# Two middle feed-forwards of a decoder trunk: from two column groups to one, with seven block products

## The chip, the cores and the metric

One core of a Trainium2 chip runs the whole kernel in one launch. The metric is device time in microseconds (us) of that core, the median of three runs.

## The reference, cut to what matters

Two layers, each feed-forward, token mixer, feed-forward, on 512 tokens of width 1024. Each sub-layer is normed, and scaled, shifted and gated by rows of a modulation that is computed from a vector `c`. All in float32.

```python
c_act = jax.nn.silu(c)
for l in range(DEPTH):                                  # DEPTH = 2
    mod = (c_act @ w_ada[l] + b_ada[l]).reshape(B, N_MOD, D_MODEL)
    sh1, sc1, gt1, sh2, sc2, gt2, sh3, sc3, gt3 = [mod[:, i, None, :] for i in range(N_MOD)]
    hn = rms_norm(h, g_ffn1[l]) * (1.0 + sc1) + sh1
    h = h + 0.5 * (1.0 + gt1) * swiglu(hn, w_ffn1_in[l], w_ffn1_out[l])
    ...                                                 # the mixer, with sh2, sc2, gt2
    hn = rms_norm(h, g_ffn2[l]) * (1.0 + sc3) + sh3
    h = h + 0.5 * (1.0 + gt3) * swiglu(hn, w_ffn2_in[l], w_ffn2_out[l])

def swiglu(x, w_in, w_out):                             # w_in 1024 x 5632, w_out 2816 x 1024
    gate, up = jnp.split(x @ w_in, 2, axis=-1)
    return (jax.nn.silu(gate) * up) @ w_out
```

The order of the sub-layers is ffn1, mix, ffn2 of layer 0, then ffn1, mix, ffn2 of layer 1, numbered n = 0 to 5. The two "middle" feed-forwards are n = 2 and n = 3, which follow each other without a mixer between.

## The kernel before

Everything is held transposed: features on the 128 partitions, tokens along the free axis. `h` is 8 tiles of 128 x 512. The normed input `hn` is 8 pairs of tiles (`hnH`, `hnL`), high and low part of each value: a float32 product is made of three matmuls in a faster format (H by H, H by L, L by H; `mm3`, `mm6`, `prod`), which accumulate in PSUM. A weight block of 128 x 1024 is loaded as `wraw`, and `split` (L103 to L105) makes `wH` by a cast on ScalarE (ACT) and `wL` by a subtraction on VectorE (DVE). `wH` and `wL` have four buffers each.

A feed-forward has 2816 = 22 x 128 inner columns, numbered j. The first four of them (in n = 0 the first eight) are computed tile by tile (`projector`), and meanwhile sums and differences of `hn` halves (P1, P2, T3, T4) are prepared. The others go in pairs p (two j each, `pair_in`): gate and up of both are made by seven block products of 24 matmuls of 256 columns in the place of eight, on sums of weight blocks. These sums come partly from DVE and partly from transfers that add to what lies in SBUF (`plus`, issued on GpSimd's (POOL) queue). Plain weight loads go through SyncE's (SP) queue.

Feed-forwards n = 0, 2 and 3 run in two groups of inner columns (`GROUPS`, 12 and 10). After each group its part of the out product is computed, eight tiles of 12 and 10 row blocks by 512 tokens, and added to `h` by DVE (`residual`). The last two tiles of the second group are computed in halves of 256 tokens by `close`, with the next norm's statistics between them, lower half of the tokens first; DVE and ACT have a fixed order there.

The last feed-forward, n = 5, runs in one group (`whole_k`): the products of the pairs are kept in `raw` tiles, and the out product is computed by seven block products (`out_strassen`, matmuls at L661) of 11 row blocks, 4 tiles and 3 matmuls, 256 columns each. Some of its weight sums come from accumulating transfers (L565), some from DVE (L606), and `finish` (L668) adds the products to `h`.

The modulation is computed by the way. `ada_steps` loads a row block of `w_ada` (512 KB) on POOL's queue, and DVE multiplies and sums it against a replicated silu(c), called `crep` (`ada_dot`, L168, a "dot" below). Each middle feed-forward computes 36 dots, 21 beside the out product of group 0 and 15 beside that of group 1; the last one computes 8, each in two halves, beside its pairs. `crep` is loaded and passed through silu in each feed-forward.

The order of instructions on each engine is found by a list scheduler from the program order; `issue_after` adds constraints, and within `manual_schedule` the named engines keep the program order. The wait of an instruction stops all that is behind it on its engine or queue.

Of the kernel before, what the change touches and what calls it, by code (L numbers as in the profile page):

```python
# [35 lines left out]
GROUPS = ((0, 12), (12, 22))  # L36
RWKV_WORK, ATT_WORK, FILL_WORK = 29.8, 15.2, 129.6
# [23 lines left out]
def trunk_kernel(ctx, tc, ins, out, layers=L, phases=("ffn1", "mix", "ffn2")):  # L61
# [107 lines left out]

    def ada_crep(pool):  # L170
        c = pool.tile([P, D], F32, name="crep", tag="crep", bufs=1)
        nc.sync.dma_start(c, ins["crep"])
        act(c, c, AF.Silu)
        return c

    def ada_steps(pool, crep, n, behind=None):
# [16 lines left out]
        del todo[:n]  # L193

# [23 lines left out]
    def norm(l, g, ish, isc, ss):  # L218
# [18 lines left out]
        def spread(sl):  # L237

            r, pt = rstd[sl.start], psum([P, T // 2], "ps_rstd", "r0" if sl.start else "x")
            for b in range(2):  # L240
                mm(pt[:, b * P : (b + 1) * P], r[:, b : b + 1].to_broadcast([P, P]), cst("ident"), start=True, stop=True)
            rstd[sl.start] = pt
# [20 lines left out]
    loads = []  # L263

# [15 lines left out]
    def projector(srcs, hn, tags, pts=None, ahead=0, ready=None):  # L280
# [8 lines left out]
        if pts is None:  # L289
            pts = [psum([P, T], "ps_mm", tag) for tag in ("mm", "mm", "r1")]  # L290
            for sl in HALVES:
                for k in range(KD):
                    for w, pt in zip(ws, pts):
                        mm3(pt[:, sl], w, k, hn[k], sl, k == 0 and sl is HALVES[0], k == KD - 1 and sl is HALVES[1])
# [77 lines left out]
    def ffn(l, w_in, w_pair, w_out, hn, im, ss, need, then, ready, first=None, late=None):  # L372
# [6 lines left out]
        with tc.tile_pool(name="act", bufs=1) as ap_:  # L379
# [3 lines left out]
            whole_k = ss is None  # L383
# [26 lines left out]
            raws_ = []  # L410

            def new_raw():
                raws_.append(ap_.tile([P, 2, 2, T], F32, name="raw", tag="raw", bufs=6))
                return raws_[-1]

            def corner(X):
                return tt(X[:, 0, hi_], X[:, 1, hi_], X[:, 0, hi_], ALU.subtract)

            def new_x(p):

                if whole_k:
                    return (new_raw() if p % 2 == 0 else raws_[-1])[:, p % 2]
# [6 lines left out]
            free_rows = [new_raw()[:, i] for _ in range(2) for i in range(2)] if whole_k else []  # L429
            raws_.clear()  # L430

            def whole(n):

                for k in (2 * n, 2 * n + 4):
                    x = free_rows.pop(0) if whole_k else ap_.tile([P, 2, T], F32, name="x", tag="act", bufs=12)
# [36 lines left out]
            def put(X, sl, x, y):  # L472
                if whole_k:
                    done_ = tt(X[:, :, sl], x, y, ALU.mult)
                    return corner(X) if sl is hi_ else done_
                tt(x, x, y, ALU.mult)
# [3 lines left out]
            def pair_in(p):  # L480
# [55 lines left out]
                put(X, hi_, up, s2)  # L536

                def rest(between=None):
                    prod(pD, hl(raw(A(1, 1), None, "last")), T4, False)
                    if between:  # L540
                        between()
                    return put(X, lo_, gate, pD)

                waiting.append(rest)

            def out_strassen(rest, raws):

                cg = small_.tile([P, KD], F32, name="cg", tag="cg")
                for c, v in ((slice(0, 4), -0.5), (slice(4, 8), 0.5)):
                    ts(cg[:, c], mod[l, im + 2][:, c], v, v, ALU.mult, ALU.add)  # L550
                pD, pF, pG = ([psum([P, 2, H2], n, t) for _ in range(2)] for n, t in (("ps_d", "x"), ("ps_f", "mm"), ("ps_g", "r0")))
                ws, NU = ins["w2s"], len(raws)
                tall = [slice(2 * u, min(2 * u + 2, NF // 2)) for u in range(NU)]
                size = [s.stop - s.start for s in tall]
                S_, ready_ = {}, {}

                def block(u, *names):
                    return ws[names[0], names[1], :, tall[u]].rearrange("p k m c -> p (k m) c")

                chain = {}  # L560

                def queued(eng, op, *args, **kw):
                    last = chain.get(eng)
# [1079 lines left out]
```

## Time and profile before

| | |
|---|---|
| runs | 1884.96, 1885.17, 1879.71 us; median 1884.96 |
| the profiled execution | 1883.92 us, span 1881.8 us, granted TensorE clock 0.999 |
| TensorE matmul (PE) | busy 99% of the span |
| TensorE weight load (PEld) | 92% |
| VectorE (DVE) | 78% |
| ScalarE (ACT) | 46% |
| GpSimd (POOL) | 8% |
| moved by DMA | 317.19 MB, mean 169 GB/s |

A busy time is that in which an engine executed something; matmuls overlap in the pipeline, and so the distance between the starts of two of them tells more than the mean duration of one. The DMA share is the mean busy share of the core's 16 DMA engines. A stretch is a piece of the span for which the profile sums all of this.

### The profile page before, as it was taken

The page shows a single profiled execution, that of the slowest core. Times are in us where ns is not written, and L with a number is a line of the kernel's source. Part 1 is how long each engine was busy: PE and PEld are TensorE (multiplying, and loading weights), DVE is VectorE, ACT ScalarE, POOL GpSimd, SP SyncE. Part 2 cuts the span into 40 slices and gives each one's busy share as a digit, 9 for nine tenths or more (in the row PEclk, how much of TensorE's full clock was granted, in tenths as well). Part 3 has the DMA queues.
Part 4 walks back from the last instruction along what each step waited for, and adds up shares of the span by engine and source line. Part 5 has one row for each costly group of instructions (what it writes and reads, how often), then busy time and mean ns, then how long its engine had stood idle before and what let it go on. Part 6 is the DMA issues. An engine that isn't in the chain of part 4 may idle for free.

```text
span 1881.8 us, 37923 instructions
## 1 busy us (share of the span) xinstructions
PE 1853.7 (99%) x15796; PEld 1733.0 (92%) x15796; DVE 1462.8 (78%) x2320; ACT 871.5 (46%) x1312; POOL 155.9 (8%) x243
## 2 busy tenths in 40 slices
PE   9999999999999999999999999999999999999999
PEld 8998899897889999899899989999878889999999
DVE  7787687858886877678787776878498768888996
ACT  4453355346432555245345524544554335555653
POOL 0101100100000010110100011110000000111120
PEclk9999999999999999999999999999999999999999
DMA  8667877521222285886817688782211315787855
GB/s 305 245 180 235 261 200 235 169 71 46 75 60 71 90 228 167 291 221 188 278 56 204 174 270 234 190 267 83 91 53 60 94 39 160 213 226 210 234 129 141
DMA packets 110028, 317.19 MB, mean 169 GB/s; under 512 B 23968, under 2 KB 29088, under 8 KB 108832
## 3 DMA queue, kind: packets, MB, share of 16 engines
q1 hardware_dynamic: 78192, 203.33, 31.6%
q0 software_dynamic: 31664, 111.43, 24.2%
q8 instruction: 124, 2.03, 0.4%
q14 instruction: 48, 0.39, 0.1%
HBM read 311.31 MB, written 3.41 MB: 167 GB/s over the span
## 4 chain that ended last, share of the span: by engine, by line
PE 83%; DVE 11%; ACT 2%; issue 2%; DMA 2%; SPq 0%; ACTq 0%; DVEq 0%
PE ps_mm L101 16%; PE ps_mm L94 8%; PE ps_mm L93 8%; PE ps_mm L95 8%; PE ps_d L467 7%; PE ps_d L469 6%; PE ps_d L468 6%; PE ps_f L469 3%; PE ps_f L467 3%; PE ps_f L468 3%; PE ps_d L661 2%; PE ps_g L469 2%; PE ps_g L467 1%; PE ps_g L468 1%; PE ps_f L661 1%
## 5 line engine op out<-in xcount | busy, mean ns | idle before, releaser
L104 ACT CAST wH<-wraw 128x1024 fp32r<-128x1024 f32 (+3 forms) x266 | 249.1, 940 | 402.0 <-PE ps_mm L94 102.2
L105 DVE TENSOR_TENSOR wL<-wraw,wH 128x1024 fp32r<-128x1024 f32 (+3 forms) x266 | 286.6, 1081 | 69.2 <-ACT wH L104 68.6
L467 PE MATMUL ps_d<-comH,wH 128*128 128x256 f32 x816 | 226.1, 277 | 1.2 <-ACT s L511 0.7
L468 PE MATMUL ps_d<-comL,wH 128*128 128x256 f32 x816 | 225.3, 276 | 0.0
L469 PE MATMUL ps_d<-comH,wL 128*128 128x256 f32 x816 | 225.2, 276 | 0.0
L93 PE MATMUL ps_mm<-actH,wH 128*128 128x512 f32 (+1 forms) x588 | 216.5, 368 | 0.0
L94 PE MATMUL ps_mm<-actL,wH 128*128 128x512 f32 (+1 forms) x588 | 216.0, 367 | 0.0
L95 PE MATMUL ps_mm<-actH,wL 128*128 128x512 f32 (+1 forms) x588 | 216.0, 367 | 0.0
L168 DVE SCALAR_TENSOR_TENSOR wada<-wada,crep 128x1024 f32<-128x1024 f32 (+1 forms) x148 | 169.4, 1162 | 48.1 <-DMA wada<-in_wadaT 47.8
L101 PE MATMUL ps_mm<-hnH,wL 128*128 128x256 f32 x976 | 199.5, 282 | 1.0 <-DVE wL L105 1.0
L101 PE MATMUL ps_mm<-hnH,wH 128*128 128x256 f32 x976 | 197.4, 282 | 0.6 <-ACT wH L104 0.3
L101 PE MATMUL ps_mm<-hnL,wH 128*128 128x256 f32 x976 | 197.2, 280 | 0.0
L104 ACT CAST wH<-sum 128x1024 fp32r<-128x1024 f32 x122 | 128.5, 1054 | 139.1 <-PE ps_d L468 66.4
L105 DVE TENSOR_TENSOR wL<-sum,wH 128x1024 fp32r<-128x1024 f32 x122 | 149.1, 1223 | 54.6 <-ACT wH L104 54.5
L101 PEld LDWEIGHTS ps_mm<-hnH,wL 128*128 128x128 f32 x976 | 149.5, 188 | 8.5 <-issue 6.6
L101 PEld LDWEIGHTS ps_mm<-hnH,wH 128*128 128x128 f32 x976 | 148.7, 188 | 8.5 <-issue 5.1
L467 PEld LDWEIGHTS ps_d<-comH,wH 128*128 128x128 f32 x816 | 153.2, 188 | 2.6 <-ACT s L511 1.7
L101 PEld LDWEIGHTS ps_mm<-hnL,wH 128*128 128x128 f32 x976 | 149.5, 188 | 5.2 <-issue 4.9
L468 PEld LDWEIGHTS ps_d<-comL,wH 128*128 128x128 f32 x816 | 153.2, 188 | 0.0
L469 PEld LDWEIGHTS ps_d<-comH,wL 128*128 128x128 f32 x816 | 153.2, 188 | 0.0
L95 PEld LDWEIGHTS ps_mm<-actH,wL 128*128 128x128 f32 x588 | 110.9, 189 | 18.3
L93 PEld LDWEIGHTS ps_mm<-actH,wH 128*128 128x128 f32 x588 | 110.9, 189 | 18.2
(474 smaller groups left out, 4716.4 us busy)
## 6 DMA issues: line engine op xcount, KB each, us to landing
wada<-in_wadaT POOLq DMA_DIRECT2D x120, 512.0 KB, 5.1
wraw<-in_wmi SPq DMA_DIRECT2D x40, 512.0 KB
wraw<-in_w2p SPq DMA_DIRECT2D x36, 512.0 KB
wraw<-in_w1p SPq DMA_DIRECT2D x32, 512.0 KB
wraw<-in_w1o SPq DMA_DIRECT2D x32, 384.0 KB
wraw<-in_w1i SPq DMA_DIRECT2D x20, 512.0 KB
wraw<-in_w1o SPq DMA_DIRECT2D x32, 320.0 KB
sum<-in_w2p SPq DMA_DIRECT2D x18, 512.0 KB
```

Of the source, the lines that this page charges most:

```text
L93: mm(acc, wH, xH, start=start, stop=False)
L94: mm(acc, wH, xL, start=False, stop=False)
L95: mm(acc, wL, xH, start=False, stop=stop)
L101: mm(acc[:, sl], w[a][:, k], x[b][:, sl], start=start and n == 0 and sl is HALVES[0], stop=stop and n == 2, skip_group_check=True)
L104: nc.scalar.copy(hi, src)
L105: return nc.vector.tensor_sub(lo, src, hi.bitcast(F32))
L168: stt(w, w, 1.0, crep, ALU.mult, ALU.mult, accum_out=out_)
L467: mm(pt[:, i], wH, x[k][0], start=start and i + k == 0, stop=False, skip_group_check=True)
L468: mm(pt[:, i], wH, x[k][1], start=False, stop=False, skip_group_check=True)
L469: last = mm(pt[:, i], wL, x[k][0], start=False, stop=k == 3, skip_group_check=True)
L661: mm(pt[m // 2][:, m % 2], w[:, 4 * k + m], x[:, y, k], start=start and u + k + n + m % 2 == 0, stop=u == NU - 1 and n == 2, skip_group_ch ...
```

## The change

Feed-forwards n = 2, 3 and 5 get a function of their own, `ffn_whole`; n = 0 keeps `ffn`, from which the code for one group is removed.

- All pairs come first, the out product last, in seven block products as in `out_strassen`. The first product is now copied by ACT from its PSUM tile into that of the third, and the sixth into that of the seventh, which accumulate on it; their separate additions to `h` go.
- In `pair_in` the a00 product is copied by ACT into the PSUM tile of the third product (which accumulates on it), in place of an addition by DVE. The loaded block a00 itself becomes the third weight sum by an accumulating transfer, in place of a second load. The order of the last two products is changed.
- The dots go to fixed places, by the table `DOTS`: in n = 2 and 3 six beside the first tiles, then 4, 4, 4, 4, 4, 4, 3, 2, 1 beside pairs 2 to 10; in n = 5 two beside each of pairs 2 to 5. Their rows go to parts of the `raw` tiles that are free at the time (`ROWS`), and a load is issued as soon as a dot has freed a buffer, up to a pair ahead.
- silu(c) is stored to DRAM once at the start (`silu_c`), and each feed-forward loads it from there.
- At the end of n = 2 and 3 the fixed order of DVE and ACT is written anew: the next norm's upper half is applied beside the last units of the seventh product, the lower half behind it, and the next stage's first tiles start with the upper half (`lead`).

The core of the diff:

```diff
+DOTS = ((0, 0, 2, 2, 2, 2), (0, 6, 4, 4, 4, 4, 4, 4, 3, 2, 1))
+ROWS = {1: (0, 1, 2, 3), 2: (0, 1, 2, 3), 3: (0, 1, 2, 3), 4: (2, 3, 4, 5), 5: (2, 3, 4, 5), 6: (4, 5, 6, 7), 7: (4, 5, 6, 7), 8: (5, 6, 7), 9: (6, 7), 10: (7,)}
...
+    def ada_plan(plan, bufs, crow):
...
+        def load(p):
+
+            for n in range(done[0], len(last)):
+                q, b, (l, i, k) = last[n]
+                if n in rows or q > p + 1 or any(last[m][1] == b for m in range(done[0], n)):
+                    continue
+                rows[n] = bufs[b]
+                nc.gpsimd.dma_start(bufs[b], ins["wadaT"][l, i, k])
+
+        def dot(p, behind=None):
...
+            with tc.issue_after(behind.ins) if behind else nullcontext():
+                ada_dot(mod[l, i][:, k : k + 1], rows[n], crow[p > 1])
...
+            done[0] += 1
+            load(p)
...
-            r, pt = rstd[sl.start], psum([P, T // 2], "ps_rstd", "r0" if sl.start else "x")
+            r, pt = rstd[sl.start], psum([P, T // 2], "ps_rstd", "r0" if sl.start and not whole_ else "x")
...
             pts = [psum([P, T], "ps_mm", tag) for tag in ("mm", "mm", "r1")]
-            for sl in HALVES:
+            first_, second_ = lead[0]
+            lead[0] = HALVES
+            for sl in (first_, second_):
...
+    def ffn_whole(l, w_in, w_pair, w_s, hn, im, ss, need, then, ready):
...
+            def pair_in(p):
+                load_rows(p)
...
+                alone, second_ = p == n_first, p == n_first + 1
+                S = raw(A(1, 0), ("sum0", "sum1")[p % 2], after_="a00")
+                nc.gpsimd.dma_start(S, A(1, 1), accum_op=ALU.add)
+                with queue_behind(order["s2"] if second_ else None):
+                    S_ = hl(S)
+                prod(pF, S_, P1, True)
+                up = half_("up")
+                taken = nc.scalar.copy(up, pF)
+                a00 = raw(A(0, 0), ("first", "third")[p % 2], "a00")
+                prod(pD, hl(a00), B11, True)
+                s1 = half_("s1") if alone else pG
+                copied = nc.scalar.copy(s1, pD)
+                tt(S, S, a00, ALU.add)
+                nc.gpsimd.dma_start(a00, A(1, 0), accum_op=ALU.add)
...
+                for f in waiting:
+                    done[0] = f()
+                waiting.clear()
+                dots(done[0], p)
+                with queue_behind(taken if alone else None):
+                    second = hl(S)
+                with queue_behind(front if alone else None):
+                    middle = prod(pD, second, P2, False)
+                s2 = half_("s2")
+                order["s2"] = nc.scalar.copy(s2, pD)
...
+                    a01 = raw(A(0, 1))
+                    right = hl(a01)
+                    prod(pG, right, B21, False)
+                gate = half_("gate")
...
+                mark = act(gate, gate if alone else pG, AF.Silu)
+                dots(mark, p)
+                tt(S, S, a01, ALU.add)
+                with queue_behind(copied if alone else None):
+                    last = hl(S)
+                prod(pF, last, B22, False)
+                mark = tt(s2, pF, s2, ALU.add)
+                act(s2, s2, AF.Silu)
+                dots(mark, p)
+                third = hl(a00)
+                prod(pD, third, T3, False)
+                mark = tt(up, pD, up, ALU.add)
+                dots(mark, p)
+                tt(X[:, :, hi_], up, s2, ALU.mult)
+                mark = corner(X)
+                dots(mark, p)
...
+                plan = (("A0", "a", pD, True, ()), ("S", "a-c", pF, True, ((1, hi_, False),)), ("A1", "b", pG, False, ((0, lo_, True),)),
+                        ("S0", "-a", pD, False, ((0, hi_, False),)), ("S1", "c", pF, False, ((0, hi_, True),)),
+                        ("S3", "d", pD, False, ((1, hi_, True),)), ("A3", "b", pG, False, ((1, lo_, True),)))
...
+                with tc.manual_schedule(engines=HAND):
+                    prepare(end - 2)
+                    ahead(0, raws[0])
+                    prepare(end - 1)
+                    ahead(1, raws[1])
+                    nothing(end - 2)
+                    nothing(end - 1)
+                    sqs = [update(5, m) for m in range(4)]
+                    prepare(end)
+                    for sq in sqs:
+                        total(sq, hi_)
+                    nothing(end)
+                    stats(hi_)
...
+                    apply(hi_, range(3))
+                    for n, m in enumerate(unit(len(units) - 1)):
+                        sq = update(6, m)
+                        apply(hi_, range(3 + n, 4 + n))
+                        total(sq, lo_)
+                        if n == 1:
+                            ahead(2, raws[2])
+                    stats(lo_)
+                    apply(hi_, range(7, KD))
+                    spread(lo_)
+                    apply(lo_, range(KD))
+                    ahead(3, raws[3])
+                    lead[0] = (hi_, lo_)
+                    return low_()
...
+        nc.sync.dma_start(silu_c[0], crep)
...
-            marks = ffn(l, ins[w + "i"], ins[w + "p"], ins[w + "o"], hn, im, nss, need, then, ready, first, late)
+            if n:
+                marks = ffn_whole(l, ins[w + "i"], ins[w + "p"], ins[w + "s"], hn, im, nss, need, then, ready)
+            else:
+                marks = ffn(l, ins[w + "i"], ins[w + "p"], ins[w + "o"], hn, im, nss, need, then, ready, first, late)
```

`prepare(t)` loads what is due at unit t and splits weights and inputs of unit t + 2; a unit is two of the 11 row blocks of one product; `update` adds a tile to `h` and squares it, `total` adds the square to the norm's sum; `ahead` loads and splits a weight block of the next stage. The file of weights for n = 2 and 3 is laid out as that of n = 5 was.

More of the change, by code (lines that the diff above doesn't have):

```diff
@@ L193, in ada_steps @@
         del todo[:n]
+    def ada_plan(plan, bufs, crow):
+        begun, last, marked = {}, [], set()
+        turns = {}
+        for p, n in enumerate(plan):
+            for _ in range(n):
+                own = ROWS[p]
+                turns[p] = turns.get(p, -1) + 1
+                last.append((p, own[(turns[p] + 2 * (p == 2 and plan[1] > 0)) % len(own)], todo.pop(0)))
+        left, loaded, done = list(range(len(last))), {}, [0]
+        rows = {}
+        def load(p):
[6 more added lines that the diff above has]
+        def dot(p, behind=None):
+            n = done[0]
+            if n == len(last) or last[n][0] != p:
+                return
+            l, i, k = last[n][2]
+            if (l, i) not in mod:
+                mod[l, i] = const.tile([P, KD], F32, name=f"mod{l}_{i}")
+            k0 = begun.setdefault((l, i), k)
+            with tc.issue_after(behind.ins) if behind else nullcontext():
+                ada_dot(mod[l, i][:, k : k + 1], rows[n], crow[p > 1])
+                if k == KD - 1 or n == len(last) - 1:
+                    v = mod[l, i][:, k0 : k + 1]
+                    tt(v, v, prm(l, "b_ada")[:, i * KD + k0 : i * KD + k + 1], ALU.add)
+            done[0] += 1
+            load(p)
+        return load, dot
     def ada_until(pool, crep, l, i):
@@ L216, in square, with norm @@
         return sq
[L218 removed]
+    def norm(l, g, ish, isc, ss, whole_=False):
         hn = [rows_of(k, ("hnH", "hnL")) for k in range(KD)]
@@ L428, in ffn @@
             rows_, sums = [], {}
-            free_rows = [new_raw()[:, i] for _ in range(2) for i in range(2)] if whole_k else []
-            raws_.clear()
             def whole(n):
                 for k in (2 * n, 2 * n + 4):
-                    x = free_rows.pop(0) if whole_k else ap_.tile([P, 2, T], F32, name="x", tag="act", bufs=12)
+                    x = ap_.tile([P, 2, T], F32, name="x", tag="act", bufs=12)
                     for i in range(2):
@@ L470, in prod, with put @@
                 return last
[L472 to L476, printed above, removed]
+            def put(X, sl, x):
                 nc.scalar.copy(X[0][:, :, sl], x)
@@ L689, in ffn, with rest @@
+                tt(up, s2, up, ALU.mult)
+                put(X, hi_, up)
+                def rest():
+                    prod(pD, hl(raw(A(1, 1))), T4, False)
+                    tt(gate, pD, gate, ALU.mult)
+                    return put(X, lo_, gate)
+                waiting.append(rest)
             turn_ = [0]
@@ L702, in ffn @@
             crep = ada_crep(ap_) if n_first == 4 else None
[L703 to L718 removed]
+            for g, (j0, j1) in enumerate(GROUPS):
                 for p in range(j0 // 2, j1 // 2):
@@ L1369, in normed @@
         g, im = what[p]
-        return norm(l, g, im, im + 1, ss)
+        return norm(l, g, im, im + 1, ss, n > 1 and seq[n - 1][1] != "mix")
     def begin(pool):
```

480 lines of the change are left out of this document (308 added, 172 removed).

## The prediction

> **What bounds the kernel now.** I read the page's span, engine and clock lines first, then the busy time of each engine in stretches cut where TensorE (PE) changes its work, then the groups by form, the chain and the waits.
>
> ```profile
> span 1881.8 us, 37923 instructions
> PE 1853.7 (99%) x15796; PEld 1733.0 (92%) x15796; DVE 1462.8 (78%) x2320; ACT 871.5 (46%) x1312; POOL 155.9 (8%) x243
> PEclk9999999999999999999999999999999999999999
> ...
> 621.20:667.06 45.86, 45.86 (x393) 45.38 (x393) 41.86 (x70) 26.50 (x39) 1.76 (x2) 1.00 0.46 137
> 667.06:743.38 76.32, 76.32 (x675) 76.32 (x673) 58.31 (x62) 43.10 (x56) 6.77 (x9) 1.00 0.70 193
> 743.38:808.67 65.29, 65.29 (x290) 54.07 (x289) 48.34 (x81) 14.95 (x18) 12.23 (x21) 1.00 0.83 271
> 808.67:904.92 96.25, 96.09 (x841) 95.69 (x840) 72.74 (x78) 53.51 (x69) 7.70 (x10) 1.00 0.74 208
> 904.92:961.02 56.10, 56.10 (x310) 49.08 (x309) 45.17 (x81) 21.13 (x34) 6.35 (x12) 1.00 0.58 194
> 961.02:1007.96 46.94, 45.92 (x395) 45.20 (x393) 39.66 (x65) 25.12 (x36) 1.98 (x3) 1.00 0.44 127
> 1595.70:1767.42 171.72, 171.72 (x1515) 171.72 (x1514) 141.32 (x181) 92.65 (x116) 25.03 (x34) 1.00 0.78 217
> 1767.42:1879.00 111.58, 109.28 (x926) 108.22 (x924) 91.73 (x144) 55.85 (x84) 16.41 (x19) 1.00 0.64 158
> ```
>
> Columns of the stretches: length, busy time (and instructions) of PE, PEld, DVE, ACT and POOL, granted clock, busy share of the DMA engines, GB/s. The first six rows are one middle feed-forward and the start of the next: first tiles, four pairs, product of group 0, five pairs, product of group 1, first tiles again. The last two are the last feed-forward, which already is in one group with seven block products: nine pairs, then the products. PE has no hole in the middle feed-forward except about 1 us at the hand-off, at clock 1.00, and DVE has slack in every stretch. So what counts is how many matmuls there are and how far apart they start; a second matter is whether DVE, the next engine, can follow a shorter PE.
>
> **The change, part by part.**
>
> *PE, out product.* A middle feed-forward spends 65.29 + 56.10 = 121.4 us in its two out stretches, 0.8 of it the next norm's small matmuls (the two rows of the chain below): 120.6. It has 22 x 8 x 3 = 528 products of 512 columns, 468 of them as 512 wide, 60 as 120 halves. The new form has 7 products x 11 row blocks x 4 tiles x 3 = 924 of 256 columns, an eighth less by columns.
>
> ```profile
> L94 PE MATMUL ps_mm<-actL,wH 128*128 128x512 f32 x468 | 182.1, 389 | 0.0
> ...
> 743.77 0.23 PE ps_mm L94
> 774.38 0.23 PE ps_mm L94
> ...
> 954.89 0.36 PE ps_ss L231 x4
> 956.42 0.44 PE ps_rstd L241 x4
> ...
> 1815.45 15.55 PE ps_d L661 x132
> 1831.00 15.55 PE ps_f L661 x132
> ...
> L467 PEld LDWEIGHTS ps_d<-comH,wH 128*128 128x128 f32 x816 | 153.2, 188 | 2.6 <-ACT s L511 1.7
> ```
>
> The mean durations of the first row overlap in the pipeline, so I don't use them. The two L94 starts are 45 triples apart: 30.61 / 135 = 0.2267 us for 512 columns (and 288 in 65.29). The block products of the last feed-forward give 15.55 / 132 = 0.1178 for 256, the form that the change uses. So 924 x 0.1178 = 108.8 us against 120.6: **-11.8 each**. On the page "TensorE: Matmul & The Clock Gate" (Back-to-back issue gap) the Trainium skill gives a sustained spacing of about 131 ns at 512 columns and 81 ns at 128, which makes narrow products dear: read between the two, about 98 ns at 256 (an estimate), 90.6 us against 69.2, so 21 us lost each. The trace disagrees at both widths, and the measurement decides. That page's other formula, N/2.4 + 2.5 ns, gives 100.9 against 113.9 and agrees in sign and size.
>
> *PE, pairs.* 76.32 + 96.25 = 172.6 us in two groups, 171.72 in one with the same 1512 matmuls (9 x 7 x 24): **-0.9 each**. With the product that is -12.7, twice: **-25.5 us** before anything that holds PE up.
>
> *DVE in the pairs.* The change takes the 36 modulation dots of each middle feed-forward out of the two out stretches, where DVE was idle for 17 and 11 us, and puts 6 beside the first tiles and 4 beside each of pairs 2 to 7, then 3, 2, 1. The rows below are one pair of the last feed-forward, groups of DVE over six of its pairs (1634 to 1748.5), two dots of a middle one, and DVE's waits in those six pairs (total, times, longest):
>
> ```profile
> 1653.08:1672.16 19.08, 19.08 (x171) 19.08 (x170) 15.50 (x20) 9.99 (x13) 2.87 (x4) 1.00 0.80 216
> ...
> L168 DVE SCALAR_TENSOR_TENSOR wada<-wada,crep 128x512 f32<-128x512 f32 x12 | 8.2, 683 | 0.0
> L521 DVE TENSOR_TENSOR gate<-ps_g,s 128x512 f32<-128x512 f32 x6 | 4.1, 683 | 0.0
> ...
> 747.40 1.22 DVE L168 SCALAR_TENSOR_TENSOR wada<-wada,crep 128x1024 f32<-128x1024 f32 x1
> 748.54 1.22 DVE L168 SCALAR_TENSOR_TENSOR wada<-wada,crep 128x1024 f32<-128x1024 f32 x1
> ...
> DVE wL L105 <- ACT wH L104: 14.1, 24, 1.0
> DVE raw L474 <- PE ps_d L469: 2.9, 6, 0.5
> DVE s L534 <- PE ps_f L469: 2.9, 6, 0.5
> DVE up L530 <- PE ps_d L469: 1.5, 6, 0.2
> ```
>
> A pair of the last feed-forward takes PE 19.08 us and DVE 15.50, with two half dots (some 0.6 each, by half of 1.14). Without them and without the gate add, which becomes an ACT copy into PSUM that the next product accumulates on, DVE has 15.50 - 1.2 - 0.6 = 13.7. Four dots, 1.14 apart in the rows above, and their bias adds make 18.3, 96% of PE's 19.08. The waits add up to 21.4 / 6 = 3.6 us a pair in which DVE now stands idle for a cast or a product. Only 0.8 remains. These waits shrink when DVE falls behind, because casts and products are then ready; with four buffers of wH and wL the splits may lag by up to three products (8 us) before PE starves. So the cost lies between 0 and 2.8 us a four-dot pair (18.3 + 3.6 - 19.08). A row of DVE at full load tells where between:
>
> ```profile
> 1784.00:1788.00 4.00, 3.73 (x32) 3.53 (x31) 4.00 (x7) 3.46 (x6) 0.00 (x0) 1.00 0.96 175
> 1788.00:1792.00 4.00, 4.00 (x36) 4.00 (x35) 4.00 (x7) 2.72 (x5) 0.00 (x0) 1.00 0.01 1
> 1808.00:1812.00 4.00, 3.22 (x29) 3.02 (x28) 4.00 (x7) 3.73 (x6) 0.00 (x0) 1.00 0.23 64
> ```
>
> With DVE full, PE lost 0 to 0.8 us of 4; over all of 1767.42 to 1879 it lost 2.3 us of 111.6 (111.58 - 109.28), 2%. I take 2.5% of the six pairs' 114.5 us: **+3 each**, toward the low end, as DVE in the pairs is still a little short of full.
>
> *DMA in the pairs.* A pair loads six blocks of 512 KB instead of seven (the a00 block is turned into the third in place by an accumulating transfer) and four rows of 512 KB: 10 x 0.524 MB in 19.08 us, 275 GB/s, against 216 now.
>
> ```profile
> 1764.00:1768.00 4.00, 4.00 (x38) 4.00 (x37) 4.00 (x8) 2.23 (x4) 2.10 (x3) 1.00 1.05 243
> 1831.00:1846.55 15.55, 15.55 (x134) 15.55 (x134) 11.86 (x19) 8.88 (x16) 5.13 (x6) 1.00 1.12 221
> ...
> third<-in_w2p POOLq DMA_DIRECT2D x18, 512.0 KB, 6.6
> rowk<-in_w2s POOLq DMA_DIRECT2D x13, 256.0 KB, 10.9
> ```
>
> The out stretch 743.38 moved 271 GB/s at a share of 0.83, mostly plain loads and rows; stretches full of accumulating transfers reach 1.05 to 1.12 at 221 to 243, and there PE wasn't held. So it fits, barely. Rows are issued as soon as a dot frees a buffer, about a pair ahead, so a dot waits for none. What is queued behind a row on POOL is the accumulate of a00; it has from the split of a00 to that of the third block, five products of 19.08 / 7 = 2.73 us or 13.6, and lands in 6.6 to 10.9: hidden, with 3 to 7 us to spare. If rows hold it for longer, the cast of the third block and with it DVE stand still. I take 0, with 1 us a pair as the bad end (12 pairs: +12). "DMA: Bandwidth & Descriptors" (Specifications) of the Trainium skill puts the HBM limit of a core at about 358 GB/s, which 275 wouldn't touch; the rows above are full at two thirds of that, so its limit isn't the one that binds here.
>
> *DVE and PE in the products and at the hand-off.* The last feed-forward's 91.73 us of DVE lose 8 updates (the first product is copied into the third's PSUM by ACT and accumulated on, and so the sixth into the seventh's) and gain 16 sums of squares, eight upper-half norm tiles of two operations, and three weight splits.
>
> ```profile
> 961.48 0.48 DVE L312 SCALAR_TENSOR_TENSOR h<-ps_mm,cg,h 128x256 f32<-128x256 f32 x1
> 961.87 0.47 DVE L251 SCALAR_TENSOR_TENSOR hn_t<-h,gmod,ps_rstd 128x256 f32<-128x256 f32 x1
> 962.26 0.48 DVE L258 SCALAR_TENSOR_TENSOR hnL<-hn_t,mod,hnH 128x256 fp32r<-128x256 f32 x1
> ```
>
> At 0.4 us each that is -3.2 + 6.4 + 6.4 + 3 x 1.14 = +13: some 105 of 108.8. PE lost 2.3 us in that stretch of the last feed-forward; I take **+2** here, bounds 0 and 5 (4.5%, the worst when two such engines stay full). At the hand-off PE now idles 46.94 - 45.92 = 1.0 us. In the new order the next stage begins with its upper half, normed beside the last units, and 72 matmuls (8.4 us) cover the lower half's sum, root and spread. But the third weight's split stands behind the second update, and DVE has 1.6 us of work per tile where PE has 9 matmuls, 1.06 us. **+0.5**, bounds -1 and +3.
>
> *The last feed-forward.* Its 8 dots become whole, two a pair in four pairs, and it loses the gate adds; PE was never short there, so nothing; at its products 8 fewer updates where DVE was full: **-1**, bounds 0 and -2. *Start:* one 512 KB store of silu(c) on SP behind the first loads, where a load queue feeds PE: **+0.5**, bounds 0 and +2; the reloads drop an ACT pass each, which nobody waits for.
>
> Sum: -25.5 + 2 x (3 + 0 + 2 + 0.5) - 1 + 0.5 = **-15**. The profiled execution took 1883.92 us beside its span of 1881.8, 1.0 below the median of the three runs: 1883.9 - 15 = **1869**.
>
> **The rivals.** (a) *DVE becomes the bound* (the other side): its 3.6 us of waits a pair persist, because each dot is queued behind a marked operation that waits for PE, and the splits of the coming products stand behind both. Twelve pairs then take 21.9 us: +33.6 in place of +6, so 1896. It decides from 2.1 us a pair (25.5 / 12). For it: 96% leaves 0.8 us. Against: the full rows above, where PE kept going. 0.13. (b) *Late transfers*, 1 us a pair: 1869 + 12 = 1881, about as before; shares of 1.05 to 1.12 speak for it, the spare of 3 to 7 us against. 0.17. (c) *Out stage and hand-off at their bad ends*, 2 x (3 + 2.5) = +11: 1880. 0.07. (d) *Narrow products cost more than they save*: with a weight load of 188 ns unhidden behind each, 924 x 0.188 = 174 us for 121, +106: 1990. The 132 in 15.55 us are of the same form and hide it: 0.01.
>
> **How the numbers follow.** The forecast, 1858 (all stalls nil) to 1875, holds 0.62. Within 0.3% (5.6 us, what runs here that spread from 1879.71 to 1885.17 can tell) means above 1879: half of (b) and (c), 0.12. Slower: (a), (d): 0.14. Faster: the rest, 0.74. The range to 1885 takes in (b) and (c) and leaves out (a), (d) and little else.
>
> **What would show it.** The out stage of a middle feed-forward at 109 to 112 us with rows of 132 in 15.55; pairs 2 to 7 at 19.1 to 19.6 us each, DVE over 18 busy; DMA near 275 GB/s there. Wrong if those pairs take over 20 us (then see whether DVE waits for ACT's cast of the a00 or row buffers, or is full), or if the first tiles after a middle feed-forward take over 49 us.

## The result and the profile after

The changed kernel takes 1914.08 us (median of four runs, 1911.23 to 1917.14), the kernel before 1885.06 on the same chip: a ratio of 1.016, with a 95% interval of 1.014 to 1.019. The forecast was 1869, with a range to 1885. The change is slower by 29 us where 15 us were to be won.

The page of the profiled execution (1911.23 us) begins thus:

```profile
span 1909.1 us, 39588 instructions
PE 1845.2 (97%) x16468; PEld 1752.5 (92%) x16468; DVE 1530.9 (80%) x2432; ACT 918.3 (48%) x1412; POOL 191.9 (10%) x281
```

PE has fallen from 99% to 97% of a longer span: it now waits. DVE rose by only two points, so a full DVE isn't what the page shows. The stretches say where. Columns as in the prediction; the rows are n = 2 (pairs, out product, first tiles of the next), n = 3 (pairs, out product, mixer and all up to the last pairs) and n = 5 (pairs, out product):

```profile
669.21:856.55 187.34, 177.73 (x1522) 175.45 (x1521) 164.51 (x216) 90.11 (x116) 29.99 (x43) 0.99 0.78 231
856.55:974.00 117.45, 112.58 (x959) 110.26 (x958) 99.57 (x160) 70.33 (x114) 17.41 (x20) 1.00 0.63 161
974.00:1019.31 45.31, 42.73 (x362) 41.90 (x361) 36.13 (x62) 21.14 (x29) 7.25 (x13) 1.00 0.63 224
1019.31:1210.91 191.60, 180.54 (x1522) 179.29 (x1521) 166.32 (x216) 90.91 (x116) 30.50 (x44) 0.96 0.79 230
1210.91:1328.40 117.49, 113.78 (x959) 111.65 (x958) 99.66 (x160) 70.03 (x114) 17.41 (x20) 0.99 0.62 160
1328.40:1618.64 290.24, 281.22 (x2993) 252.36 (x2991) 225.00 (x448) 130.51 (x248) 6.68 (x13) 1.00 0.25 79
1618.64:1797.73 179.09, 175.16 (x1522) 174.56 (x1521) 136.13 (x156) 91.25 (x116) 18.64 (x23) 0.99 0.68 186
1797.73:1909.10 111.37, 106.11 (x918) 105.01 (x916) 86.85 (x132) 57.70 (x87) 16.54 (x19) 1.00 0.62 152
```

The out products and the hand-off became shorter, as forecast. The pairs became longer in all three feed-forwards: 187.3 and 191.6 us where 76.32 + 96.25 stood before, and 179.1 where 171.7 stood. The clock is below 1.00 in these stretches, and of the other rows only in the out product of n = 3. Two rows of the waits (who waited, at which line, for what: us in total, times, longest) name what is new:

```profile
DVE raw L170 <- DMA raw<-in_wadaT: 53.1, 15, 6.1
PE ps_f L730 <- DVE wL L107: 10.0, 7, 4.4
```

A dot (L170) stood 15 times in front of a row of modulation weights that hadn't landed. Behind it on DVE stands the split (L107) that makes the low part of the next weights, and PE starts its next product only with that. The chain at the start of the pairs of n = 3 shows one such wait from end to end (start us, length, what):

```profile
1011.37 0.01 POOLq L217
1011.39 10.27 DMA raw<-in_wadaT
...
1021.68 0.04 DVE raw L170
...
1022.92 1.15 DVE wL L107
...
1024.11 0.39 PE ps_f L730
...
1024.88 0.21 PE ps_f L728
1025.09 0.21 PE ps_f L729
...
1028.38 0.12 PE ps_f L730
```

The row is asked for at 1011.4, as soon as a dot that ended at 1011.1 has left its buffer, and lands 10.3 us later, the dot runs, the split runs, and only then does PE go on. For 3.4 us after that its matmuls are 0.21 us apart and not 0.12. The stretches of that place, 1 us each, give the reason:

```profile
1020.00:1021.00 1.00, 0.00 (x0) 0.00 (x0) 0.56 (x3) 0.00 (x0) 0.22 (x1) 1.00 1.02 410
1024.00:1025.00 1.00, 0.89 (x6) 0.89 (x7) 1.00 (x2) 0.00 (x0) 0.64 (x1) 0.84 1.07 401
1025.00:1026.00 1.00, 1.00 (x7) 1.00 (x7) 1.00 (x2) 0.00 (x0) 0.00 (x0) 0.50 0.89 315
1027.00:1028.00 1.00, 1.00 (x7) 1.00 (x6) 1.00 (x3) 0.00 (x0) 0.72 (x1) 0.50 0.96 234
1028.00:1029.00 1.00, 1.00 (x10) 1.00 (x9) 1.00 (x2) 0.47 (x1) 0.00 (x0) 0.96 1.13 225
```

The granted clock fell to 0.50 after the hole and came back 3.4 us later. So a wait of DVE can be paid twice: as a hole in PE, and as slow matmuls behind it. How much each counts is worked out below from the best kernel's rows.

Two theories were open here. A: DVE has no slack left in the pairs, and any delay shows (rival (a) of the prediction). B: the rows come too late, or the dots too early (rival (b), though through waits and not through full DMA engines).

### The profile page after: what moved, and what is told of

Its sections match the earlier page's. It is cut to its first block, busy times and chain, and to the rows that moved or that the text cites. A ratio compares the mean times of both kernels' runs of the same rounds, so it can differ in the third digit from the quotient of the medians.

```text
span 1909.1 us, 39588 instructions
## 1 busy us (share of the span) xinstructions
PE 1845.2 (97%) x16468; PEld 1752.5 (92%) x16468; DVE 1530.9 (80%) x2432; ACT 918.3 (48%) x1412; POOL 191.9 (10%) x281
## 4 chain that ended last, share of the span: by engine, by line
PE 45%; DVE 21%; DMA 11%; issue 7%; ACT 3%; POOL 1%; SPq 0%; POOLq 0%; DVEq 0%; ACTq 0%
PE ps_mm L103 7%; DVE wL L107 6%; DMA raw<-in_wadaT 5%; PE ps_d L930 5%; PE ps_f L930 3%; PE ps_g L930 2%; PE ps_d L728 2%; PE ps_d L730 2%; PE ps_d L729 2%; PE ps_mm L96 2%; PE ps_mm L97 2%; PE ps_mm L95 2%; ACT wH L106 2%; PE ps_f L730 1%; PE ps_f L728 1%
## 5 line engine op out<-in xcount | busy, mean ns | idle before, releaser
L106 ACT CAST wH<-wraw 128x1024 fp32r<-128x1024 f32 (+2 forms) x210 | 207.2, 988 | 310.5 <-PE ps_mm L103 63.6
L107 DVE TENSOR_TENSOR wL<-wraw,wH 128x1024 fp32r<-128x1024 f32 (+2 forms) x210 | 238.9, 1140 | 54.5 <-ACT wH L106 54.1
L107 DVE TENSOR_TENSOR wL<-sum,wH 128x1024 fp32r<-128x1024 f32 x153 | 186.7, 1220 | 41.3 <-ACT wH L106 41.0
L728 PE MATMUL ps_d<-comH,wH 128*128 128x256 f32 x648 | 180.7, 279 | 3.2 <-DVE up L799 2.1
L729 PE MATMUL ps_d<-comL,wH 128*128 128x256 f32 x648 | 180.0, 278 | 0.0
L930 PE MATMUL ps_d<-xs,wH 128*128 128x256 f32 x792 | 137.2, 278 | 0.0
L930 PEld LDWEIGHTS ps_d<-xs,wH 128*128 128x128 f32 x792 | 120.4, 190 | 0.1
L170 DVE SCALAR_TENSOR_TENSOR raw<-raw,crow 128x1024 f32<-128x1024 f32 x68 | 82.8, 1218 | 45.2 <-DMA raw<-in_wadaT 45.2
L930 PE MATMUL ps_d<-xs,wL 128*128 128x256 f32 x396 | 110.4, 279 | 3.8 <-DVE wL L107 3.8
L930 PE MATMUL ps_f<-xs,wH 128*128 128x256 f32 x528 | 90.3, 276 | 0.0
L217 POOL DMA_DIRECT2D raw<-in_wadaT x80 | 44.7, 572 | 427.0 <-DVE hn_t L293 192.6
```

Of the source, the lines that this page charges most:

```text
L106: nc.scalar.copy(hi, src)
L107: return nc.vector.tensor_sub(lo, src, hi.bitcast(F32))
L170: stt(w, w, 1.0, crep, ALU.mult, ALU.mult, accum_out=out_)
L217: nc.gpsimd.dma_start(bufs[b], ins["wadaT"][l, i, k])
L728: mm(pt[:, i], wH, x[k][0], start=start and i + k == 0, stop=False, skip_group_check=True)
L729: mm(pt[:, i], wH, x[k][1], start=False, stop=False, skip_group_check=True)
```

## The experiments

All ratios are against runs of the kernel before on the same chip (medians of 1885.0 to 1888.1 us). Where three rounds were run, the interval is given; the others are one run each.

### Is it the dots or the rows?

The dots read the resident silu(c) in place of the rows, and no rows are loaded, so that the modulation isn't that of the reference; DVE's work stays:

```diff
-                nc.gpsimd.dma_start(bufs[b], ins["wadaT"][l, i, k])
...
-                ada_dot(mod[l, i][:, k : k + 1], rows[n], crow[p > 1])
+                c = crow[p > 1]
+                stt(rows[n], c, 1.0, c, ALU.mult, ALU.mult, accum_out=mod[l, i][:, k : k + 1])
```

> In the changed feed-forwards the dots stay, but each multiplies the resident silu(c) tile with itself and no row is loaded; the modulation of these sub-layers is left out. Late rows (a dot at the head of DVE's queue waits for its row): pairs of the middle feed-forwards fall from 187 and 192 us to 171 to 175 each, of the last from 179 to 172 to 174, no dip of the clock in them, time near 1875. DVE full (rival a): the dots' work is all there, so pairs stay at 183 to 190 and the time at 1900 or more. Traffic (rows crowd the DMA engines): as with late rows here; the rows without dots tell the two apart.

The reverse: rows are loaded in step with a small constant write that stands in for each dot:

```diff
-                nc.gpsimd.dma_start(bufs[b], ins["wadaT"][l, i, k])
+                with tc.issue_after(marks[0].ins) if marks else nullcontext():
+                    nc.gpsimd.dma_start(bufs[b], ins["wadaT"][l, i, k])
...
-                ada_dot(mod[l, i][:, k : k + 1], rows[n], crow[p > 1])
+                marks[:] = [nc.vector.memset(mod[l, i][:, k : k + 1], 0.01)]
```

> The rows are loaded, paced by the same places in DVE's order, but each dot is replaced by a constant written into one column and nothing reads the rows; the modulation is left out. Late rows: nothing waits for a row any more, pairs 171 to 174 us, time near 1872. Traffic: weights still come late, pairs stay over 180, time over 1895. DVE full: DVE is relieved by 36 x 1.14 us a middle feed-forward, pairs 171 to 174.

And neither rows nor dots (the load is left out, the constant stays):

> Neither rows nor dots; the modulation is left out. All theories: pairs at the 171.7 us of the last feed-forward before. What is left above the forecast is then the cost of the out products and the hand-off alone: by the changed kernel's stretches (116.3 us a middle feed-forward for 924 matmuls) the time is about 1872; if those stretches were slow only as a consequence of late rows, about 1858.

Measured: 1870.32 us with dots and no rows, 1891.17 with rows and no dots, 1866.54 with neither; the kernel before 1885.02. The stretches of the pairs of n = 2 and 3 in the kernel with dots and no rows:

```profile
671.50:844.40 172.90, 172.70 (x1519) 172.43 (x1518) 162.43 (x213) 91.81 (x116) 16.24 (x19) 1.00 0.65 171
1004.30:1177.10 172.80, 172.80 (x1522) 172.73 (x1521) 162.30 (x210) 91.78 (x116) 16.20 (x19) 1.00 0.66 171
```

DVE is busy for 162 of 173 us, as it is in the changed kernel (164 to 166), and PE has holes of 0.2 us at most. With neither rows nor dots these pairs take 172.8 and 172.9 us, so the dots by themselves cost next to nothing. That ends theory A: all the dots fit, and without the rows the time is what the prediction said, within 2 us. It doesn't yet tell late rows from the traffic that rows bring, since both went.

The kernel with rows and no dots was slow for another reason than the changed one. Its pairs (184.3 and 186.2 us) hold one long hole each, of 9.6 and 10.1 us. The clock stands at 0.50 for some 4 us behind it, and elsewhere the pairs run at full speed. The rows of POOL before the first hole, and the cast that waited:

```profile
688.09 0.54 POOL L219 DMA_DIRECT2D raw<-in_wadaT  x1 [10.50 <-DMA raw<-in_wadaT]
...
692.72 0.53 POOL L219 DMA_DIRECT2D raw<-in_wadaT  x1 [1.54 <-DMA raw<-in_wadaT]
699.91 0.90 POOL L765 DMA_DIRECT2D third<-in_w2p  x1 [1.08 <-issue]
710.00 1.04 ACT L106 CAST wH<-third 128x1024 fp32r<-128x1024 f32 x1 [16.06 <-DMA third<-in_w2p]
```

With no dot to read it, a row buffer is refilled when its last row has landed, and the loads themselves wait on POOL. The accumulating transfer of the third block (L765) stands behind them, and ACT's cast then waits for it. The experiment made this wait itself, so of theory B it shows only that, away from the hole, the rows' traffic doesn't slow PE.

### Which rows are late: the rotation of the buffers

In the changed kernel the dots of n = 2 that waited end their waits at 669.0, 700.9, 722.9, 763.0, 799.7 and 820.8 us: the sixth dot beside the first tiles, then the first dots of pairs 3, 4, 6, 8 and 9. The change hands out the buffers of `ROWS` in turn within a pair and begins anew at each pair, so that a pair's first dot can get a buffer that was freed two dots earlier. The edit gives each row the buffer that has been free for longest:

```diff
-                own = ROWS[p]
-                turns[p] = turns.get(p, -1) + 1
-                last.append((p, own[(turns[p] + 2 * (p == 2 and plan[1] > 0)) % len(own)], todo.pop(0)))
+                used = {b: m for m, (_, b, _) in enumerate(last)}
+                last.append((p, min(reversed(ROWS[p]), key=lambda b: used.get(b, -1)), todo.pop(0)))
```

> Rows and dots as in the change, but each dot takes the buffer of its pair's set that was freed longest ago, so at least four dots (in pairs 9 and 10 three and two) lie between the freeing of a buffer and the dot that reads its next row, where it was two at pairs 3, 4, 6 and 9. Late rows: the waits at the first dots of these pairs go, the one at the fifth dot beside the first tiles (3 to 4 us of DVE) stays; pairs 176 to 180 in the middle and 175 in the last, time 1885 to 1893. DVE full or traffic: the same work and bytes, time 1905 to 1917.

Measured: 1903.13 us, 11 under the changed kernel, but above the 1885 to 1893 that was expected for late rows. All the rows in n = 2 in which DVE still waited for one:

```profile
675.91 1.23 DVE L170 SCALAR_TENSOR_TENSOR raw<-raw 128x1024 f32<-128x1024 f32 x1 [5.27 <-DMA raw<-in_wadaT]
691.73 1.23 DVE L170 SCALAR_TENSOR_TENSOR raw<-raw,crow 128x1024 f32<-128x1024 f32 x1 [2.18 <-DMA raw<-in_wadaT]
737.21 1.22 DVE L170 SCALAR_TENSOR_TENSOR raw<-raw,crow 128x1024 f32<-128x1024 f32 x1 [0.54 <-DMA raw<-in_wadaT]
```

The later pairs are nearly free of it. The early ones aren't, and the pairs of n = 2 and 3 still take 184 to 185 us.

### The start of a feed-forward, by counts and queues

The next four kernels keep the oldest buffer and go for the early wait. First, four dots beside the first tiles in place of six (four buffers serve them), one dot more at each of pairs 8 and 9, and an earlier request for the first rows of n = 5:

```diff
-DOTS = ((0, 0, 2, 2, 2, 2), (0, 6, 4, 4, 4, 4, 4, 4, 3, 2, 1))
+DOTS = ((0, 0, 2, 2, 2, 2), (0, 4, 4, 4, 4, 4, 4, 4, 4, 3, 1))
...
-                        if not j:
-                            load_rows(0)
+                        if not j or j == 2 and not plan_[1]:
+                            load_rows(j // 2)
...
-                        for _ in range({2: 2, 3: 4}.get(j, 0)):
+                        for _ in range({2: 2, 3: 2}.get(j, 0)):
```

> The whole computation, with as many dots and rows as in the change, only earlier rows: each dot takes the buffer of its set that was freed longest ago; four dots instead of six beside the first tiles (4 in each of pairs 2 to 8, then 3, 1), so that each of the first four reads a row that was loaded before the stage; and in the last feed-forward the first rows are asked for one tile group earlier. Late rows: no dot finds its row missing by more than 1 us, pairs 172 to 176 us in all three feed-forwards, no clock dip in them, time 1870 to 1880, under the kernel before. DVE full or traffic: bytes and DVE's work are those of the change, time 1900 or more.

On top of it, two sums of the out product are loaded earlier (`"S1": 3, "S3": 3` becomes `"S1": 4, "S3": 6`):

> As the kernel with earlier rows, and in the out product the accumulating transfers of the sixth product are issued six units ahead instead of three, those of the fifth four instead of three. If the gap of some 1.9 us in the sixth product, and the dip of the clock that followed it, came from those transfers landing late, the gap goes and the time is 2 to 8 us lower than with earlier rows alone; if the gap is DVE's queue at that place, the time is the same within 2 us.

Or two rows fewer still at the start (`DOTS = ((0, 0, 0, 2, 2, 2, 2), (0, 4, 2, 4, 4, 4, 5, 5, 4, 3, 1))`):

> The whole computation, as with earlier rows, and the dots moved away from the second pair: 4 beside the first tiles, then 2, 4, 4, 4, 5, 5, 4, 3, 1 in the middle; in the last feed-forward two in each of pairs 3 to 6 instead of 2 to 5. The one wait that is left with earlier rows (6 us at a dot of pair 2, whose row stood in POOL's queue behind the accumulate of the next weight sum) loses its dot. Late rows: pairs 172 to 176 us everywhere, no clock dip in the pairs, time 1873 to 1883. If pairs 5 to 7 with 18.3 to 19.5 us of DVE work are then the limit (DVE full), pairs 178 or more and time 1890 or more.

Or the rows on SP's queue in place of POOL's (`nc.sync.dma_start` in `load`), past the accumulating transfers that POOL issues in order:

> As with earlier rows, with the rows issued on SP's queue instead of POOL's: no row stands behind an accumulating transfer any more, but weight loads now stand behind rows that wait for a dot. If POOL's queue is what holds the rows, the 6 us wait at pair 2 shrinks to under 2, pairs 174 to 178, time 1880 to 1890; if it is the transfer itself under the load of the early pairs, landing stays near 10 us and the time within 4 us of that with earlier rows; if weights are held behind rows, over 1905.

| kernel | median us | ratio, 95% interval | pairs n = 2, 3, 5 |
|---|---|---|---|
| counts | 1898.58 | 1.0063 (1.0044 to 1.0083) | 182.1, 185.0, 178.6 |
| counts, sums earlier | 1895.38 | 1.0047 (1.0028 to 1.0067) | 184.3, 184.0, 179.3 |
| counts, fewer at the start | 1902.03 | 1.0073 (1.0047 to 1.0099) | 185.6, 186.9, 180.6 |
| counts, rows on SP | 1896.33 | 1.0044 (1.0032 to 1.0057) | 181.6, 180.9, 183.6 |

None of the first, third and fourth reaches the time expected if its edit cured the late rows (1870 to 1880, 1873 to 1883, 1880 to 1890), and none of the four removes the early wait. The queue of POOL isn't its cause, since with the rows on SP the dots wait 18.4 us in 5 waits, against 19.1 in 5. Earlier sums are worth nothing that can be told (the intervals overlap). The kernel with fewer rows at the start tells why. In its n = 5 the table has no dot before pair 3, but DVE ran four dots beside the first tiles and early in pair 2, the last of them ahead of a split of pair 2 for which PE then waited 4.5 us:

```profile
1605.33 1.22 DVE L170 SCALAR_TENSOR_TENSOR raw<-raw,crow 128x1024 f32<-128x1024 f32 x1
...
1616.50 1.23 DVE L170 SCALAR_TENSOR_TENSOR raw<-raw,crow 128x1024 f32<-128x1024 f32 x1 [8.00 <-DMA raw<-in_wadaT]
...
1617.99 1.22 DVE L107 TENSOR_TENSOR wL<-sum,wH 128x1024 fp32r<-128x1024 f32 x1
```

These are dots of later pairs, drawn forward. In `pair_in`, the second dot of a pair is `dots(mark, p)` with `mark = act(gate, ...)`: an instruction of ScalarE. The constraint orders what stands on the mark's own engine, and the dot runs on VectorE, so that nothing held it; the list scheduler put it where DVE seemed idle, in front of splits that PE needs.

### Dots held in their places

One edit: the second dot stands behind VectorE's split of the fourth product's weights (`low[0]` is the subtraction of the last `hl`).

```diff
-                mark = act(gate, gate if alone else pG, AF.Silu)
-                dots(mark, p)
+                act(gate, gate if alone else pG, AF.Silu)
+                dots(low[0], p)
```

It was added to the kernel with counts, to the changed kernel alone, to the kernel with fewer rows at the start, and to the kernel with the oldest buffer alone. In the first three expectations "theory A" means that dots drawn forward are the cause, and "theory B" that the rows come late whatever the order on DVE:

> e6_row_timing with one edit: the second dot of each pair is placed behind VectorE's split of the fourth product's weights (a VectorE instruction) and not behind ScalarE's silu, which does not order VectorE's list, so that no dot is drawn ahead of its place. Theory A (dots drawn too early in VectorE's fixed order stand ahead of the split that TensorE needs, and wait there for rows that could not have come yet): the 6 us wait at the early pairs goes, PE gaps over 2 us in pairs go, pairs of the two middle ffn 173 to 177 us, total 1872 to 1884, under the kernel before. Theory B (the rows themselves come late because an ffn asks for its first eight together while the pair weights use the same DMA engines, whatever the order on VectorE): the wait only moves to another dot, pairs stay at 181 to 186, total 1894 to 1903.

> The changed kernel with that one edit alone: buffers in the change's rotation and its counts of rows. Theory A as far as it goes: the waits at dots drawn early go, those at the first dots of pairs 3, 4, 6 and 9, whose buffer was freed only two dots ahead, stay: 1890 to 1905, pairs 180 to 187. If the placing is worth nothing by itself: 1909 to 1917, pairs 187 to 192 as in the changed kernel. If the placing is all of it: 1870 to 1882.

> e8_fewer_early (two rows fewer at the start of each ffn) with the same edit. Theory A: fewer rows in flight at the start and every dot in its place, so the start's wait goes too: pairs 172 to 176, 1868 to 1880, a few us under e10. Theory B: as e8, 1899 to 1905, with one wait of 3 to 6 us left per ffn.

> The changed kernel with the two edits that are about order alone: rows go to the buffer freed longest ago (e3) and the second dot of a pair stays in its place on VectorE (e11); the change's counts of rows, and its later request in the last ffn, are kept. Alone the two gave 1903 each (11 and 11 us under the changed kernel) and with the counts 1871.75. If the two edits cover separate waits and the counts are worth nothing: 1870 to 1880 and pairs 173 to 177 in the two middle ffn. If the counts carry part of it (a first dot of pair 3 with six rows asked for at pair 2): 1882 to 1893, with one wait of 2 to 5 us left at an early pair of each ffn and pairs 177 to 183.

Beside them stands what the dots waited for rows in each profiled execution, in us and times; the pairs are of that execution too:

| kernel | median us | ratio, 95% interval | DVE's wait for rows | pairs n = 2, 3, 5 |
|---|---|---|---|---|
| the change | 1914.08 | 1.0161 (1.0137 to 1.0186) | 53.1, 15 | 187.3, 191.6, 179.1 |
| dots in place | 1902.97 | 1.0095 (1.0074 to 1.0116) | 44.2, 13 | 188.5, 191.1, 173.1 |
| oldest buffer | 1903.13 | 1.0096 (one run) | 24.2, 8 | 184.4, 185.2, 178.3 |
| oldest buffer, counts | 1898.58 | 1.0063 (1.0044 to 1.0083) | 19.1, 5 | 182.1, 185.0, 178.6 |
| dots in place, oldest buffer, fewer at the start | 1890.01 | 1.0022 (1.0009 to 1.0035) | 19.0, 6 | 182.5, 181.5, 173.1 |
| dots in place, oldest buffer | 1880.75 | 0.9986 (0.9974 to 0.9998) | 8.6, 3 | 175.5, 179.4, 173.2 |
| **dots in place, oldest buffer, counts** | **1871.75** | **0.9926 (0.9903 to 0.9949)** | 2.0, 2 | 173.0, 174.4, 173.0 |

The last row beats both kernels, and with all its rows it is within 2 us of the kernel without rows (1870.32). Its steps don't add up one by one: each of the first two edits alone gives 11 us, both together 33; with buffers and counts in place, the dots' places are worth 27 (1898.58 to 1871.75). The pairs show why. In n = 5 the dots' places are the whole cause: that edit alone takes the pairs from 179.1 to 173.1 us, and the buffers alone leave them at 178.3. In n = 2 and 3 there are two causes, of which either is enough: with the dots in place alone the same six dots of n = 2 wait as in the changed kernel, so the pairs stay at 188.5 and 191.1 us where 180 to 187 was expected. With oldest buffer and counts but free dots, dots still stood in front of the splits (first three rows; the last two are the same kernel with the dots in place):

```profile
677.71 1.23 DVE L107 TENSOR_TENSOR wL<-sum,wH 128x1024 fp32r<-128x1024 f32 x1
684.89 1.22 DVE L170 SCALAR_TENSOR_TENSOR raw<-raw,crow 128x1024 f32<-128x1024 f32 x1 [5.96 <-DMA raw<-in_wadaT]
...
689.47 1.22 DVE L107 TENSOR_TENSOR wL<-sum,wH 128x1024 fp32r<-128x1024 f32 x1
```

```profile
672.83 1.23 DVE L107 TENSOR_TENSOR wL<-sum,wH 128x1024 fp32r<-128x1024 f32 x1 [2.90 <-ACT wH L106]
673.98 1.22 DVE L170 SCALAR_TENSOR_TENSOR raw<-raw,crow 128x1024 f32<-128x1024 f32 x1
```

Above, a dot of an early pair holds DVE for 6 us and the next split comes 11.8 us after the one before it. Below, the split comes first and the dot finds its row there.

With buffers and places but without the counts, three waits are left, all of dots beside the first tiles, of which the fifth and sixth must wait for buffers that the first two have just left:

```profile
669.37 1.22 DVE L170 SCALAR_TENSOR_TENSOR raw<-raw 128x1024 f32<-128x1024 f32 x1 [3.92 <-DMA raw<-in_wadaT]
1004.70 1.23 DVE L170 SCALAR_TENSOR_TENSOR raw<-raw 128x1024 f32<-128x1024 f32 x1 [3.46 <-DMA raw<-in_wadaT]
1007.25 1.22 DVE L170 SCALAR_TENSOR_TENSOR raw<-raw 128x1024 f32<-128x1024 f32 x1 [1.24 <-DMA raw<-in_wadaT]
```

These 8.6 us are all the waits for rows in that kernel, and the best one, which has four dots there, is 9 us faster. The pairs of n = 5 take 173.2 us there without the earlier request, against 173.0 with it, so that request is worth nothing once the dots are in place.

The kernel with fewer rows at the start missed its expectation: it puts five dots into each of pairs 6 and 7, and in n = 2 the first dots of pairs 7, 8 and 9 wait 1.53, 2.89 and 6.18 us again. A row needs its lead in every pair, not at the start alone.

## Why the prediction was wrong

These rows of the best kernel stand against those of the changed one (n = 2: pairs, out product, first tiles; n = 3: pairs, out product; n = 5: pairs, out product), and behind them one pair of its n = 2:

```profile
668.30:841.30 173.00, 173.00 (x1523) 172.86 (x1523) 160.64 (x214) 91.74 (x116) 31.50 (x45) 1.00 0.87 253
841.30:955.30 114.00, 111.20 (x958) 109.61 (x957) 99.23 (x160) 70.19 (x114) 16.58 (x19) 1.00 0.64 162
955.30:999.90 44.60, 42.67 (x362) 41.86 (x362) 39.09 (x65) 21.16 (x29) 7.28 (x13) 1.00 0.64 226
999.90:1174.30 174.40, 173.39 (x1523) 173.00 (x1522) 162.67 (x213) 91.81 (x116) 30.58 (x44) 1.00 0.87 254
1174.30:1289.20 114.90, 111.86 (x958) 109.78 (x957) 99.32 (x160) 70.22 (x114) 17.46 (x20) 1.00 0.64 162
1579.40:1752.40 173.00, 172.84 (x1522) 172.64 (x1521) 137.61 (x158) 91.48 (x116) 17.61 (x22) 1.00 0.69 181
1752.40:1865.00 112.60, 107.81 (x918) 106.86 (x917) 86.87 (x132) 57.41 (x87) 16.57 (x19) 1.00 0.62 151
```

```profile
750.00:769.00 19.00, 19.00 (x170) 19.00 (x169) 17.79 (x24) 9.95 (x12) 3.95 (x6) 1.00 0.90 259
```

For n = 3 and the mixer the kernel before has one row, 587.74 us:

```profile
1007.96:1595.70 587.74, 578.28 (x5133) 530.69 (x5132) 448.42 (x749) 265.53 (x426) 37.74 (x63) 1.00 0.48 145
```

| us against the profile before | forecast | the change | best kernel |
|---|---|---|---|
| start to the pairs of n = 2 | +0.5 | +2.2 | +1.2 |
| n = 2: pairs | +2.1 | +14.8 | +0.4 |
| n = 2: out product, hand-off, first tiles | -9.3 | -5.6 | -9.7 |
| n = 3 with the mixer | -7.2 | +11.6 | -8.2 |
| n = 5 | -1 | +4.4 | -0.5 |
| sum | -15 | +27 | -17 |

(n = 2 before: 76.32 + 96.25 for the pairs, 65.29 + 56.10 + 46.94 for the rest; n = 5 before: 171.72, and 114.38 to the end of the span. The columns are single executions, for the best kernel the fastest of its four, 1866.87 us; its median of 1871.75 is 14 us under the kernel before, not 17.)

**The step that failed** is "DMA in the pairs", and in it one sentence: "Rows are issued as soon as a dot frees a buffer, about a pair ahead, so a dot waits for none." It read the lead of a load off the bound in the code (up to a pair ahead) and not off the buffers. A row can be asked for no sooner than the dot that last used its buffer, in DVE's real order, and in the changed kernel that left less than the 10.3 us that a row took at 1011 to 1021. The real order differed as well: the prediction took each dot to be queued behind a marked operation (rival (a)), and the second dots of the pairs weren't held. Rows land no faster in the best kernel, by a median of 6.7 us from issue to landing in both; what it has is lead. The forecast's 0 became 53 us of waits on DVE. They cost the pairs of all three feed-forwards 37.6 us: 558.0 in the changed kernel, 520.4 in the best one. Of these 23.4 are holes (length less PE's busy time: 24.6 against 1.2), and 14.2 are PE being counted busy for longer on the same matmuls. The lower clock accounts for some 9 of these, an estimate from the starts in the trace: in the pairs of the changed kernel 86 matmuls at 0.50 start 0.21 us apart and not 0.11. The rest lies in short gaps and at the edges of the holes.

The lower clock had no term at all. The Trainium skill ("TensorE: Matmul & The Clock Gate", Part 1: The HAM clock gate) says that the clock halves when TensorE idles through a window of some 3.4 us, and comes back after a busy one. The 0.50 and the 3.4 us of this trace agree. It differs in what sets it off: at 707 us the clock fell although PE had been busy for 1.7 us of the five before (0.42, 0.00, 0.50, 0.00 and 0.79 in stretches of 1 us), so no idle stretch of 3.4 us was needed. Nor does every hole set it off: the clock stayed at 1.00 behind the one at 821.4 to 823.2 us.

**DMA bandwidth** was judged rightly: in the best kernel a pair moves 259 GB/s at a share of 0.90, forecast as 275 and "fits, barely", and PE is busy throughout. Rival (b) was right that transfers would be late, but for want of lead, not of bandwidth, and its price of 12 us over both was too low: against the best kernel the pairs of n = 2 and 3 lost 14.3 and 17.2 us. In the changed kernel, the DMA share of these pairs is 0.78 and 0.79 against 0.87: the transfers had room.

**DVE in the pairs** (+3 each) was too dear. A four-dot pair keeps DVE busy for 17.8 of 19.0 us (forecast 18.3 of 19.08), and the pairs take 173.0 and 174.4 us, against 173.0 in n = 5 with its eight dots. Rival (a), DVE as the bound, which the prediction took for nearly all of the danger on the slow side, is refuted by the kernel that keeps the dots and drops the rows. The 0.9 us a feed-forward that one group was to save in the pairs didn't come: even with neither rows nor dots they take 172.8 us, against 172.6 before.

**The out product** was right in the sum of the stage and not in its parts. Matmuls were closer than 0.1178 us (the last section has the rows), but the stage had 2.8 us of holes even in the best kernel and products at its ends that weren't back to back, and so took 114 to 115 us, not 109 to 112. The hand-off gave more back: the first tiles behind n = 2 take 44.6 us and not 47.4. That the sum comes out near the forecast is in part luck, errors that cancel.

**What would show it** did its work: the pairs of n = 2 and 3 took 20.8 and 21.3 us each, over its 20, and it named waits for row buffers among the places to look, which is what the trace then showed.

## What to carry to other kernels

The lead of a load is the time from the last use of its buffer, in the consumer engine's real order, to the next use; compare it with the longest landing of such a load in the busiest place, not with the mean. An instruction that may wait for a transfer belongs behind, not ahead of, the work on its engine that the bounding engine needs, and a constraint given on another engine's instruction may not hold it there: read the order off the trace. When one edit removes few of the waits, another cause may stand behind the same wait, so try the edits together before dropping either.

## What the hardware showed that was not expected

The same matmul form (block products, 256 columns) ran at two spacings at a granted clock of 1.00: 14.96 / 132 = 0.1133 us in the changed kernel (first two rows), and in the best kernel 14.05 / 124 = 0.1133 in the first product of n = 5 and 15.55 / 132 = 0.1178 in a later one of the same stretch (last two rows), as in the kernel before.

```profile
904.08 14.96 PE ps_d L930 x132
919.04 14.96 PE ps_f L930 x132
```

```profile
1752.61 14.05 PE ps_d L929 x124
1813.72 15.55 PE ps_f L929 x132
```

It is worth 4 us in 924 matmuls. No run here was made to find what sets it; it stays open.

Where the first rows of n = 3 are under way, the DMA engines moved 401 to 410 GB/s (stretches at 1020 and 1024 us above), half more than the 271 at a share of 0.83 that the prediction started from and more than the limit of a core that it quoted, and a single row of 512 KB took 10.3 us in it. At 1028 us the engines are as full (1.13 against 1.02) and move 225 GB/s. So a full share doesn't tell the rate; what sets the rate was not isolated by a run here.
